# First norm of a hybrid encoder layer: the 16 modulation column tiles that it uses are summed over their inputs by TensorE in PSUM instead of by VectorE, ScalarE and Pool

## The chip, the core and the metric

The kernel runs on one core of one Trainium2 chip. A core has five engines that run their own instruction streams and meet at semaphores: TensorE (PE in the profile, its weight loads PEld), VectorE (DVE), ScalarE (ACT), GpSimd or Pool (POOL) and SyncE (SP), whose stream here issues most of the DMAs. The metric is the device time of one execution in microseconds; lower is better. The median of three runs of the kernel before is 2705.27 us (2701.91 to 2705.51).

## The reference

One layer of a bidirectional encoder on a sequence of 1024 tokens with 1024 features, float32. What the change touches is the first line of the layer: a modulation vector is computed from the condition `c`, and its first two sixths shift and scale the first norm. All four mixers start from `u`.

```python
cond = jax.nn.silu(c.astype(jnp.float32))              # (1, 1024)
mod = cond @ ada_w[l] + ada_b[l]                       # 1024 x 6144 weights
sh1, sc1, gt1, sh2, sc2, gt2 = jnp.split(mod[:, None, :], 6, axis=-1)
u = _rmsnorm(h, norm1_g[l]) * (1.0 + sc1) + sh1
p_rw, p_ml, p_lru, p_hg, p_gate = _split(u @ w_in[l], IN_SPLITS)
...
h = h + gt1 * (merged @ w_out[l])
u2 = _rmsnorm(h, norm2_g[l]) * (1.0 + sc2) + sh2
h = h + gt2 * _conv_ffn(u2, ...)
return _rmsnorm(h, final_g)
```

## The kernel before

Features lie on the 128 partitions, tokens along the free dimension. A column tile is 128 columns of `ada_w`, so `mod` is a tile of 128 partitions by 48 columns (column g holds column tile g: 0 to 7 are the shift, 8 to 15 the scale of the first norm). The condition after SiLU is `sc`, 128 by 8: column k holds inputs 128k to 128k+127.

The stage of the change is a loop of four steps (i = 0 to 3) in `run`. Step i makes the four column tiles 2i, 2i+1, 8+2i and 8+2i+1, and with them the feature tiles k = 2i and 2i+1 of `u`. In a step:

- `ada` loads, for two neighbouring column tiles at a time, all 1024 inputs of their 256 columns in one DMA of 1 MB (tile `ada_w`, 128 x 8 x 256). The weighted sum over the eight k is split: VectorE multiplies and accumulates k = 0 to 4 into one `ada_acc` (lines 1386 and 1388), ScalarE multiplies k = 5 to 7 (line 1397), and Pool adds these to a second `ada_acc` (line 1399).
- `ada_end` sums the 128 partitions of both accumulators with TensorE: the accumulator is the weight operand, a column of ones the moving one, and the result is one PSUM column (line 1414). VectorE adds the bias and writes `mod` (line 1417).
- `norm1` makes `g1` from `mod` and the norm's gain (lines 1459, 1460), transposes the normalised tokens `n1_x` for each k with TensorE (line 1446; first half to the PSUM bank `ps`, second half to `pt`), and scales and shifts out of PSUM into `n1_u`, first half by VectorE (1449), second by ScalarE (1451). ScalarE rounds this to `uh` (205), and VectorE or Pool takes the rest into `ul` (206).
- `proj_part` adds feature tiles to three column blocks of `u @ w_in` whose PSUM banks (`big`, `pc`, `pa`, `py`) stay open through the loop. Each product of two float32 matrices is three matmuls of 128 x 512 (lines 126 to 128: high by high, high by low, low by high), so that each k costs 18 matmuls: 144 in all.

The bank `pt` serves both `ada_end` and the second half of `norm1`; it has one buffer. After the loop come `load_cols`, `rw_params`, and then the first branch's projections with the LRU units (`lru`, `lru_unit`). Instructions are not in the order of the code: a list scheduler that runs when the kernel is built orders each engine's stream, so that a change in one stage also moves instructions in later ones. Matmul weights (`w_raw`) are split into `w_hi` (VectorE, line 119) and `w_lo` (Pool, line 120) through three buffers each.

Of the kernel before, what the change touches and what calls it, by code (L numbers as in the profile page):

```python
# [18 lines left out]
P = 128  # L19
T = 1024  # L20
ADD, SUB, MUL, MAX, MIN = ALU.add, ALU.subtract, ALU.mult, ALU.max, ALU.min


class K:
# [1351 lines left out]
    def ada(self, g0, g1, wp, G=4, bufs=2, ks=8, pend=None):  # L1376
# [3 lines left out]
        for g in range(g0, g1, G):  # L1380
# [24 lines left out]
            else:  # L1405
                pend.append((g, accs))

    def ada_end(self, pend, tag, G):
        nc = self.nc
        pt = self.ps([P, 512], tag)  # L1410
        for i, (g, accs) in enumerate(pend):
            for x in range(G):
                for q, acc in enumerate(accs):
                    nc.tensor.matmul(pt[:, G * i + x:G * i + x + 1], lhsT=acc[:, P * x:P * x + P], rhs=self.ones,
                                     start=(q == 0), stop=(q == len(accs) - 1))
        for i, (g, _) in enumerate(pend):
            nc.vector.tensor_tensor(self.mod[:, g:g + G], pt[:, G * i:G * i + G], self.c("ada_b", g, G), op=ADD)
# [48 lines left out]
    def run(self):  # L1466
        nc, a, tc = self.nc, self.a, self.tc
# [14 lines left out]
        with ExitStack() as es:  # L1482
            wp = es.enter_context(tc.tile_pool(name="st", bufs=1, reuse_waits="tile"))
            self.load_cols([("c", V("c")), ("ada_b", V("ada_b")), ("norm1_g", V("norm1_g"))], "D", wp)
            nc.scalar.activation(self.sc, self.c("c", 0, 8), AF.Silu)
            self.norm1_load(wp)
            self.ptags = [("big", "big"), ("pc", "pc"), ("pa", "py")]
            for i in range(4):
                pend = []
                with tc.high_priority(offset=self.AP):  # L1490
                    for g in (2 * i, 8 + 2 * i):
                        self.ada(g, g + 2, wp, 2, 8, self.ADK0, pend)
                    self.ada_end(pend, "pt", 2)
                ks = range(2 * i, 2 * i + 2)
                if i == 0:
                    self.norm1_stats(wp)
                    self.pres = [self.proj_start(self.win(c)) for c in (P * 12, 1792 + 1552, 1792 + 1552 + 512)]
                self.norm1(wp, ks)
                if i:
                    for pre in self.pres:  # L1500
                        self.proj_part(pre, self.PK)
                self.PK = ks
            self.load_cols([(n, V(n)) for n in ("norm2_g", "rw_mu", "rw_w0", "rw_a0", "rw_kk", "rw_ka")] +
                           [("rw_rk", a["rw_rk"].rearrange("o (j two) n -> (o j) (two n)", two=2))] +
                           [(n, V(n)) for n in ("rw_lnw", "rw_lnb", "ml_norm", "lru_conv_w", "lru_conv_b", "lru_ba",
                                                "lru_bx", "lru_lam", "hg_lb", "hg_norm")], "A", wp)
            fw = a["ffn_conv_w"].rearrange("o k (j p) -> o k j p", p=P)
            self.load_cols([("cw0", fw[0, 0]), ("cw1", fw[0, 1])], "B", wp)
            self.load_cols([("cw2", fw[0, 2]), ("cb", V("ffn_conv_b"))], "C", wp)
# [27 lines left out]
        with ExitStack() as es:  # L1537
            wp = es.enter_context(tc.tile_pool(name="hg", bufs=1, reuse_waits="tile"))
# [6 lines left out]
            for j in range(4):  # L1545
# [16 lines left out]
                for i in range(2):  # L1562
                    pt = self.ps([P, 4, P])
# [15 lines left out]
        with ml as es:  # L1579
# [8 lines left out]
            with ExitStack() as e2:  # L1588
                wp = e2.enter_context(tc.tile_pool(name="mlp", bufs=1, reuse_waits="tile"))
# [14 lines left out]
                w = self.wsplit_sb(wpad, 8)  # L1604
# [8 lines left out]
            wp = es.enter_context(tc.tile_pool(name="ml", bufs=1, reuse_waits="tile"))  # L1613
            self.filler = iter(())
            hs, q, kk = {}, {}, {}
# [50 lines left out]
        for n in (0, 3, 1, 2):  # L1666
# [6 lines left out]
            for jt in range(8):  # L1673
                sgt = self.t(mp, [P, T], "sgt", bufs=3)
                nc.sync.dma_start(out=sgt, in_=dG[8 * n + jt])
                w = self.wsplit(a["w_branch"][0, n, :, P * jt:P * jt + P], 4)
# [32 lines left out]
        wp = es.enter_context(tc.tile_pool(name="wo", bufs=1, reuse_waits="tile"))  # L1709
# [73 lines left out]
        wp = es.enter_context(tc.tile_pool(name="ffu", bufs=1, reuse_waits="tile"))  # L1783
# [147 lines left out]
        wp = self.pool("ff")  # L1931
# [22 lines left out]
        g = 0  # L1954
        while g + GR < NF:
            nx = [hidden(f) for f in range(g + GR, min(NF, g + 2 * GR))]
            down(g, GR, fs)
            fs, g = nx, g + GR
# [4 lines left out]
        w = []  # L1963
# [35 lines left out]
        pt = self.ps([P, 512])  # L1999
# [13 lines left out]
        for jt in range(8):  # L2013
# [9 lines left out]
            for k in range(jt if jt > 3 else 0, jt + 1) if jt >= 3 else ():  # L2023
                for i, (n, pt, ss) in enumerate(tl):
                    nc.tensor.matmul(ss[:, 0:1], lhsT=sqs[k][:, P * i:P * i + P], rhs=onesP, start=(k == 0), stop=(k == 7))
                    nc.tensor.matmul(pt[k // 4][:, P * (k % 4):P * (k % 4) + P], lhsT=hT[k][:, P * n:P * n + P],
                                     rhs=dg[:, k, :], start=True, stop=True)
# [88 lines left out]
```

## Time and profile before

| | us |
|---|---|
| median of three runs | 2705.27 (2701.91 to 2705.51) |
| the profiled execution, its own time | 2707.24 |
| its span (first to last instruction) | 2705.4 |
| TensorE busy in the span | 2501.7 (92%) |
| VectorE busy | 1768.4 (65%) |
| Pool busy | 1148.6 (42%) |
| ScalarE busy | 919.5 (34%) |

Shares over the whole span say little on one stage. The trace is therefore read in stretches, which are given from the start of the span: what each engine does there, what an engine waited for, and how fast TensorE's matmuls follow each other. TensorE runs at one of two clock levels; the column PEclk gives the granted share of the full one, and the step from one matmul's start to the next one's shows it too.

### The profile page before, as it was taken

To read this page: it belongs to the slowest core of one execution; us is meant where nothing else is said; L and a number is where in the kernel's file an instruction comes from. 1 tells how busy PE (TensorE), PEld (TensorE's weight loads), DVE (VectorE), ACT (ScalarE), POOL (GpSimd) and SP (SyncE) were. 2 spreads that over 40 slices of the span, in tenths; PEclk is the share of its full clock that TensorE was granted. 3 is DMA by queue.
4 is the path that set the end of the run, shared out by engine and by line. 5 is a ranking of instruction groups with operands and counts; after the bars stand their busy time and mean duration, and the time that the engine had idled before them with its cause. 6 is when DMAs were issued, how large, how long until landed. Compare 5 with 4: busy or idle time off the path is not lost.

```text
span 2705.4 us, 46888 instructions
## 1 busy us (share of the span) xinstructions
PE 2501.7 (92%) x18573; PEld 2010.5 (74%) x18573; DVE 1768.4 (65%) x2878; ACT 919.5 (34%) x1656; POOL 1148.6 (42%) x1150
## 2 busy tenths in 40 slices
PE   5999887899999999799989989999999999999998
PEld 4777666667777777588777777788777888888887
DVE  7667765776776652655563668367479999886344
ACT  4355542333333332343332342111235444442002
POOL 3654453433443323742221365367423444445332
PEclk9999998999999999899999989999999999999999
DMA  6422253444443423321111544555543222216222
GB/s 215 132 73 68 74 152 91 114 105 112 101 118 92 114 72 117 110 54 44 40 40 29 142 150 158 182 188 160 175 133 113 75 90 74 90 56 209 82 78 79
DMA packets 403173, 290.78 MB, mean 107 GB/s; under 512 B 121290, under 2 KB 365304, under 8 KB 402952
## 3 DMA queue, kind: packets, MB, share of 16 engines
q1 hardware_dynamic: 363976, 248.37, 31.7%
q10 hardware_dynamic: 38976, 39.40, 4.4%
q8 instruction: 146, 2.39, 0.4%
q14 instruction: 75, 0.61, 0.1%
HBM read 223.93 MB, written 63.77 MB: 106 GB/s over the span
## 4 chain that ended last, share of the span: by engine, by line
PE 53%; DVE 20%; issue 5%; DMA 3%; ACT 3%; POOL 2%; SPq 1%; ACTq 0%; DVEq 0%; POOLq 0%
PE pbig L126 8%; PE pbig L128 7%; PE pbig L127 7%; DVE rw_pr L1000 3%; PE ppc L128 2%; PE ppc L126 2%; PE ppc L127 2%; DVE s L1848 2%; PE ppy L126 1%; PE ppy L127 1%; PE ppy L128 1%; PE ppa L126 1%; PE ppa L127 1%; PE ppa L128 1%; DVE w_lo L1841 1%
## 5 line engine op out<-in xcount | busy, mean ns | idle before, releaser
L120 POOL TENSOR_TENSOR w_lo<-w_raw,w_hi 128x512 fp32r<-128x512 f32 x276 | 383.5, 1390 | 757.9 <-DVE w_hi L119 269.7
L126 PE MATMUL pbig<-uh,w_hi 128*128 128x512 f32 x1200 | 501.6, 419 | 20.4 <-ACT w_hi L117 8.5
L128 PE MATMUL pbig<-uh,w_lo 128*128 128x512 f32 x1200 | 479.1, 401 | 4.8 <-POOL w_lo L120 4.1
L127 PE MATMUL pbig<-ul,w_hi 128*128 128x512 f32 x1180 | 472.8, 401 | 0.0
L126 PEld LDWEIGHTS pbig<-uh,w_hi 128*128 128x128 f32 x1200 | 229.6, 192 | 86.5 <-ACT gt L1234 17.1
L128 PEld LDWEIGHTS pbig<-uh,w_lo 128*128 128x128 f32 x1200 | 230.4, 192 | 58.1 <-POOL w_lo L120 6.7
L127 PEld LDWEIGHTS pbig<-ul,w_hi 128*128 128x128 f32 x1180 | 227.2, 193 | 41.2 <-issue 1.1
L119 DVE CAST w_hi<-w_raw 128x512 fp32r<-128x512 f32 x216 | 135.3, 628 | 138.5 <-PE pbig L127 81.9
L128 PE MATMUL ppc<-uh,w_lo 128*128 128x512 f32 x352 | 139.3, 399 | 3.7 <-DVE w_lo L120 2.1
L126 PE MATMUL ppc<-uh,w_hi 128*128 128x512 f32 x352 | 138.3, 397 | 1.7 <-DVE w_hi L119 1.2
L127 PE MATMUL ppc<-ul,w_hi 128*128 128x512 f32 x332 | 131.1, 395 | 0.0
L126 PE MATMUL ppa<-uh,w_hi 128*128 128x512 f32 x216 | 86.2, 399 | 5.6 <-DVE w_hi L119 5.6
L128 PE MATMUL ppa<-uh,w_lo 128*128 128x512 f32 x216 | 85.4, 395 | 0.9 <-POOL w_lo L120 0.8
L126 PE MATMUL ppy<-uh,w_hi 128*128 128x512 f32 x216 | 85.7, 397 | 0.0
L128 PE MATMUL ppy<-uh,w_lo 128*128 128x512 f32 x216 | 84.8, 393 | 0.0
L117 ACT CAST w_hi<-w_raw 128x512 fp32r<-128x512 f32 x74 | 45.7, 618 | 112.3 <-PE pbig L127 52.0
L127 PE MATMUL ppa<-ul,w_hi 128*128 128x512 f32 x204 | 82.5, 404 | 0.0
L1839 ACT CAST w_hi<-s 128x512 fp32r<-128x512 f32 x80 | 49.4, 618 | 97.0 <-PE pbig L127 18.8
L127 PE MATMUL ppy<-ul,w_hi 128*128 128x512 f32 x208 | 82.2, 395 | 0.0
L128 PEld LDWEIGHTS ppc<-uh,w_lo 128*128 128x128 f32 x352 | 66.7, 190 | 20.8 <-DVE w_lo L120 2.6
L126 PEld LDWEIGHTS ppc<-uh,w_hi 128*128 128x128 f32 x352 | 67.1, 191 | 17.5 <-DVE w_hi L119 2.1
L1388 DVE SCALAR_TENSOR_TENSOR ada_acc<-ada_w,sc,ada_acc 128x256 f32<-128x256 f32 x112 | 71.9, 644 | 2.4
(790 smaller groups left out, 6219.1 us busy)
## 6 DMA issues: line engine op xcount, KB each, us to landing
w_raw<-in_w_in_dram SPq DMA_DIRECT2D x172, 256.0 KB
ada_w<-in_ada_w_dram SPq DMA_DIRECT2D x24, 1024.0 KB
s_raw<-in_ffn_up_dram SPq DMA_DIRECT2D x80, 256.0 KB
dG<-gt ACTq DMA_DIRECT2D x64, 256.0 KB
sgt<-dG SPq DMA_DIRECT2D x32, 512.0 KB
rw_in<-dIn SPq DMA_DIRECT2D x32, 384.0 KB
w_raw<-in_ffn_down_dram SPq DMA_DIRECT2D x44, 256.0 KB
dF<-cv SPq DMA_DIRECT2D x22, 512.0 KB
```

The source lines that it names most:

```text
L117: nc.scalar.copy(hi, raw[:, k0:k0 + m])
L119: nc.vector.tensor_copy(out=hi, in_=raw[:, k0:k0 + m])
L120: (nc.gpsimd if self.wlo == "p" else nc.vector).tensor_tensor(lo, raw[:, k0:k0 + m], hi.bitcast(F32), op=SUB)
L126: nc.tensor.matmul(pt, lhsT=wh, rhs=uh, start=start, stop=False)
L127: nc.tensor.matmul(pt, lhsT=wh, rhs=ul, start=False, stop=False)
L128: nc.tensor.matmul(pt, lhsT=wl, rhs=uh, start=False, stop=stop)
L1000: nc.vector.tensor_tensor(p4[:, y], l[:, y, i:i + m].unsqueeze(2).to_broadcast([64, m, n, n]), r[:, y].rearrange("p k j -> p j k").unsquee ...
L1388: nc.vector.scalar_tensor_tensor(acc, w[:, k, :], self.sc[:, k:k + 1], acc, op0=MUL, op1=ADD)
L1839: nc.scalar.copy(hi, x)
L1841: (nc.gpsimd if self.st_n % self.SL[1] < self.SL[0] else nc.vector).tensor_tensor(lo, x, hi.bitcast(F32), op=SUB)
L1848: (nc.gpsimd if i in self.SP else nc.vector).tensor_tensor(o, x, y, op=op)
```

## The change

The eight DMAs, `mod` and all that follows stay. The sums over k of the 16 column tiles are made by TensorE: the 128 x 128 block of `ada_w` for input tile k and a column tile is the weight operand, column k of `sc` is the moving one (128 x 1), and eight such matmuls add up in one PSUM column. The column-by-column work of VectorE, ScalarE and Pool and the sums with ones are gone for these tiles. The later 32 column tiles keep the old way.

```diff
+    def ada_pe(self, g, G, wp, pt):
+
+        nc = self.nc
+        w = self.t(wp, [P, 8, P * G], "ada_w", bufs=8)
+        nc.sync.dma_start(out=w, in_=self.a["ada_w"][0, :, P * g:P * (g + G)].rearrange("(k p) c -> p k c", p=P))
+        for x in range(G):
+            for k in range(8):
+                nc.tensor.matmul(pt[:, x:x + 1], lhsT=w[:, k, P * x:P * x + P], rhs=self.sc[:, k:k + 1],
+                                 start=(k == 0), stop=(k == 7))
+        nc.vector.tensor_tensor(self.mod[:, g:g + G], pt[:, :G], self.c("ada_b", g, G), op=ADD)
...
             for i in range(4):
-                pend = []
                 with tc.high_priority(offset=self.AP):
-                    for g in (2 * i, 8 + 2 * i):
-                        self.ada(g, g + 2, wp, 2, 8, self.ADK0, pend)
-                    self.ada_end(pend, "pt", 2)
+                    pt = self.ps([P, 512], "pt")
+                    for q, g in enumerate((2 * i, 8 + 2 * i)):
+                        self.ada_pe(g, 2, wp, pt[:, 4 * q:])
```

In the changed kernel the lines behind the new function have numbers that are larger by 11: the transposes of line 1446 stand at 1457, `mod` of the new function at 1417. On TensorE, at the end of step 0's first transposes (`pps` is the bank `ps`, `ppt` the bank `pt`), stand before:

```order
L1446 MATMUL pps_229<-ident_73,n_x_33_112 128x128
L1414 MATMUL ppt_153<-ones_79,ada_acc_39_127 128x1
L1414 MATMUL ppt_153<-ones_79,ada_acc_40_133 128x1
L1414 MATMUL ppt_153<-ones_79,ada_acc_39_127 128x1
L1414 MATMUL ppt_153<-ones_79,ada_acc_40_133 128x1
L1414 MATMUL ppt_153<-ones_79,ada_acc_42_141 128x1
L1414 MATMUL ppt_153<-ones_79,ada_acc_43_147 128x1
L1414 MATMUL ppt_153<-ones_79,ada_acc_42_141 128x1
L1414 MATMUL ppt_153<-ones_79,ada_acc_43_147 128x1
L1446 MATMUL ppt_235<-ident_73,n_x_34_113 128x128
```

and in the changed kernel at the same place:

```order
L1457 MATMUL pps_229<-ident_73,n_x_33_112 128x128
L1415 MATMUL ppt_125<-sc_78,ada_w_126 128x1 x16
L1415 MATMUL ppt_125<-sc_78,ada_w_145 128x1 x16
L1457 MATMUL ppt_235<-ident_73,n_x_34_113 128x128
L1457 MATMUL ppt_235<-ident_73,n_x_35_114 128x128
```

Two bursts of 16 matmuls, one for each DMA, take the place of eight matmuls, and the same transposes follow. In step 1 the eight matmuls of line 1414 stand nearly together behind `pps_300`; in the changed kernel the first burst stands there, and the second one inside the projections, here with its neighbours:

```order
L126 MATMUL ppc_223<-uh_12_82,w_hi_349 128x512
L127 MATMUL ppc_223<-ul_20_90,w_hi_349 128x512
L1415 MATMUL ppt_258<-sc_78,ada_w_278 128x1 x16
L128 MATMUL ppc_223<-uh_12_82,w_lo_350 128x512
L127 MATMUL ppa_224<-ul_19_89,w_hi_367 128x512
```

In steps 1 to 3 each step has on TensorE, in this order, 6 matmuls of line 126, a burst, 19 matmuls of lines 126 to 128, a burst, 11 more, and 16 transposes. Further on, where the first branch and the LRU unit begin, VectorE's stream is also in another order. Before, from the first `lru_a` to the third weight tile `w_hi_1096`:

```order
L815 CAST lru_a_201_777<-lru_th_200_774 128x1024
L262 SCALAR_TENSOR_TENSOR lru_xc_836<-lru_xb_798,colsA_635,lru_xc_836 128x1024
L732 TENSOR_TENSOR rw_kk_734<-rw_kk_734,rw_q_735 128x1024
L815 CAST lru_a_204_789<-lru_th_203_786 128x1024
L119 CAST w_hi_1023<-w_raw_1021 128x512
L262 SCALAR_TENSOR_TENSOR lru_xc_836<-lru_xb_798,colsA_635,lru_xc_836 128x1024
L203 CAST lru_w_210_841<-lru_w_830 128x512
L119 CAST w_hi_1090<-w_raw_1088 128x512
L806 TENSOR_TENSOR lru_s_199_767<-rw_kk_734,lru_s_198_766 128x1024
L228 TENSOR_TENSOR lru_e_757<-lru_e_757,lru_m_758 128x8
L229 TENSOR_SCALAR lru_C_759<-lru_e_757 128x8
L119 CAST w_hi_1096<-w_raw_1094 128x512
```

and in the changed kernel:

```order
L815 CAST lru_a_185_777<-lru_th_184_774 128x1024
L262 SCALAR_TENSOR_TENSOR lru_xc_836<-lru_xb_798,colsA_635,lru_xc_836 128x1024
L815 CAST lru_a_188_789<-lru_th_187_786 128x1024
L262 SCALAR_TENSOR_TENSOR lru_xc_836<-lru_xb_798,colsA_635,lru_xc_836 128x1024
L119 CAST w_hi_1023<-w_raw_1021 128x512
L732 TENSOR_TENSOR rw_kk_734<-rw_kk_734,rw_q_735 128x1024
L203 CAST lru_w_194_841<-lru_w_830 128x512
L806 TENSOR_TENSOR lru_s_183_767<-rw_kk_734,lru_s_182_766 128x1024
L228 TENSOR_TENSOR lru_e_757<-lru_e_757,lru_m_758 128x8
L119 CAST w_hi_1090<-w_raw_1088 128x512
L229 TENSOR_SCALAR lru_C_759<-lru_e_757 128x8
L119 CAST w_hi_1096<-w_raw_1094 128x512
```

The same twelve instructions stand in both; the second weight tile `w_hi_1090` has moved behind `lru_s` and `lru_e`, and the last row is the same.

## Rows read from the trace of the kernel before

**Rows 1.** The page: busy time, share of the span and instructions.

```profile
PE 2501.7 (92%) x18573; PEld 2010.5 (74%) x18573; DVE 1768.4 (65%) x2878; ACT 919.5 (34%) x1656; POOL 1148.6 (42%) x1150
```

**Rows 2.** Groups of instructions, 25 to 80 us: busy us, mean ns, idle before.

```profile
L1388 DVE SCALAR_TENSOR_TENSOR ada_acc<-ada_w,sc,ada_acc 128x256 f32<-128x256 f32 x32 | 22.6, 713 | 0.7
L1399 POOL TENSOR_TENSOR ada_acc<-ada_acc,ada_w 128x256 f32<-128x256 f32 x16 | 12.8, 804 | 24.1 <-ACT ada_w L1397 23.5
...
L1386 DVE TENSOR_SCALAR ada_acc<-ada_w,sc 128x256 f32<-128x256 f32 x8 | 3.7, 466 | 0.0
```

**Rows 3.** Timeline: start, duration, engine, instruction, wait and its releaser; step 0.

```profile
25.19 0.51 ACT L1397 ACTIVATE ada_acc<-ada_w,sc 128x256 f32<-128x256 f32 x1 [0.84 <-DMA ada_w<-in_ada_w_dram]
...
28.21 0.51 ACT L1397 ACTIVATE ada_acc<-ada_w,sc 128x256 f32<-128x256 f32 x1 [1.72 <-DMA ada_w<-in_ada_w_dram]
...
31.65 1.78 PEld L1414 LDWEIGHTS ppt<-ones,ada_acc 128*128 128x128 f32 x8 [1.25 <-DVE ada_acc L1388]
...
34.03 0.21 DVE L1417 TENSOR_TENSOR mod<-ppt,colsD 128x2 f32<-128x2 f32 x2
...
35.52 0.78 ACT L1451 ACTIVATE n_u<-ppt,mod,g 128x512 f32<-128x512 f32 x1
...
36.33 1.05 ACT L205 CAST uh<-n_u 128x1024 fp32r<-128x1024 f32 x1
...
37.57 1.20 PE L126 MATMUL pbig<-uh,w_hi 128*128 128x512 f32 x2
```

**Rows 4.** Timeline of TensorE: ones-matmuls of steps 1, 2 and 3.

```profile
40.77 1.62 PE L1414 MATMUL ppt<-ones,ada_acc 128*128 128x1 f32 x14
...
56.75 1.87 PEld L1414 LDWEIGHTS ppt<-ones,ada_acc 128*128 128x128 f32 x16
...
69.44 1.88 PE L1414 MATMUL ppt<-ones,ada_acc 128*128 128x1 f32 x16
```

**Rows 5.** Timeline: TensorE's waits in the stage, and matmuls of 128 x 512.

```profile
50.81 1.09 PE L1446 MATMUL ppt<-ident,n_x 128*128 128x128 f32 x4 [2.63 <-DVE mod L1417]
...
68.88 0.50 PE L126 MATMUL ppa<-uh,w_hi 128*128 128x512 f32 x1 [0.48 <-DVE w_hi L119]
...
71.76 0.63 PE L128 MATMUL pbig<-uh,w_lo 128*128 128x512 f32 x1
72.19 0.63 PE L127 MATMUL pbig<-ul,w_hi 128*128 128x512 f32 x1
...
88.57 0.39 PE L127 MATMUL ppa<-ul,w_hi 128*128 128x512 f32 x1
...
89.25 0.40 PE L128 MATMUL ppy<-uh,w_lo 128*128 128x512 f32 x1
```

**Rows 6.** Stretches, TensorE alone: length, busy us, PEclk, DMA share, GB/s.

```profile
50.00:60.00 10.00, 9.19 (x50) 0.83 0.04 11
...
70.00:80.00 10.00, 10.00 (x48) 0.83 0.21 54
71.00:72.00 1.00, 1.00 (x5) 0.55 0.77 191
```

**Rows 7.** Stretches of small matmuls later: busy PE, PEld, DVE, ACT, POOL, PEclk.

```profile
1592.00:1596.00 4.00, 4.00 (x16) 3.32 (x16) 1.15 (x4) 1.93 (x3) 0.48 (x1) 0.50 0.32 87
...
1600.00:1604.00 4.00, 4.00 (x17) 3.32 (x17) 1.70 (x3) 0.81 (x2) 1.29 (x2) 0.50 0.65 204
```

**Rows 8.** Line 1414's instructions: count, duration ns least/median/greatest.

```profile
L1414 PEld LDWEIGHTS ppt<-ones,ada_acc x64: 187/192/339, 28.6 to 71.0; 128*128 128x128 f32 x64
```

**Rows 9.** Timeline, TensorE and VectorE, where the first branch begins.

```profile
95.95 1.00 DVE L259 TENSOR_SCALAR lru_xc<-lru_xb,colsA 128x1024 f32<-128x1024 f32 x1 [5.58 <-POOL lru_xb L237]
...
111.07 0.41 DVE L119 CAST w_hi<-w_raw 128x512 fp32r<-128x512 f32 x1
...
111.62 0.47 PE L126 MATMUL ppa<-uh,w_hi 128*128 128x512 f32 x1 [4.01 <-DVE w_hi L119]
...
117.13 0.41 DVE L119 CAST w_hi<-w_raw 128x512 fp32r<-128x512 f32 x1
```

## Prediction

> **What bounds the kernel now.** The page comes first: TensorE is busy in 92% of the span, VectorE in 65% [rows 1]. That says only that time given to TensorE is likely to show at the end. The stage of the change has to be read alone, because there the shares are others.
>
> The groups of instructions from 25 to 80 us give the work that the change removes: VectorE spends 22.6 + 3.7 = 26.3 us on the sums over k, Pool 12.8 us [rows 2]. Pool's price does not matter, since it waited 24.1 us for ScalarE in the same rows. VectorE's matters only where TensorE waited for it, which the timeline tells. In step 0 it did: two DMAs land at 25.2 and 28.2, the sums end, TensorE adds up the partitions, and `mod` is written at 34.03; ScalarE's share of `u` starts at 35.52, `uh` at 36.33, and the first matmul of the projections at 37.57 [rows 3]. In the three other steps TensorE waited 2.63 us for step 1's `mod`, and 0.48 us for a weight tile [rows 5]. That is all that it waited there for longer than a few tenths: the last matmul of the three projections starts at 89.25 [rows 5], so the stage from first to last matmul takes 52.1 us, and TensorE fills it but for those 3.1 us.
>
> It does not fill it at one rate. Matmuls of 128 x 512 follow each other at 0.68/3 = 0.227 us at 88.57 to 89.25, but at 0.43 us at 71.76 [rows 5]; the granted clock reads 0.55 from 71 to 72 and 0.83 over each of the stretches 50 to 60 and 70 to 80 [rows 6]. A mean of 0.83 over 10 us is 3.4 us at half rate, the lower of the two levels (1.2 instead of 2.4 GHz), and 1.7 us lost, twice. In step 0 I go by the steps from one weight load to the next: eight in 1.78 us are 0.222 us each [rows 3], against 1.87/16 = 0.117 us at 56.75 [rows 4]. That is the lower level too.
>
> So the stage is TensorE's, with one early wait for VectorE. The change takes the work from the engine that has room and gives it to the one that has little.
>
> **The change part by part.**
>
> *Price of a burst.* The new matmul has the form of the old one with ones: 128 x 128 float32 weights, 128 x 1 moving. The trace counts 64 records of line 1414 for the 32 matmuls of this stage [rows 8], two each; a burst of 16 matmuls is 32 records. At the full level that is 32 x 0.117 = 3.74 us, at the lower one 32 x 0.222 = 7.12 us. The weight load sets it: its duration goes from 187 to 339 ns [rows 8], and a column of output costs next to nothing.
>
> Here a rule says less. The Trainium skill (TensorE: Matmul & The Clock Gate, LDWEIGHTS) puts a weight load at its 128 columns over 1.2 GHz, about 107 ns, whatever the array does; by that a burst would be an estimated 3.4 us at either level and the sum below about 9 us smaller. This trace disagrees at the lower level, with 0.222 us a step.
>
> *Step 0.* TensorE has idled before 25.2 and is at the lower level, where it was in the same place before. Two bursts are 14.24 us. The second one's first matmul also waits for VectorE's addition of the first one's bias (both write one PSUM tile), which costs about what lies between the old loads' end, 31.65 + 1.78 = 33.4, and `mod` [rows 3]: 0.6 us, and 0.6 us more to the second `mod`. So `mod` comes at 25.2 + 14.24 + 1.2 = 40.6 instead of 34.03: **+6.6**. The bounds are nothing gained on the lower rate, and the full rate for both bursts (2 x 3.38 us less). What is queued behind `mod` on VectorE is `g1`, `n_u` and `ul`, and TensorE's transposes into `pt` wait for it; the 3.54 us from `mod` to the first projection matmul [rows 3] stay.
>
> *Steps 1 to 3.* Six bursts at the full level, 22.4 us, in place of three times 1.87 us [rows 4]: **+16.8**. The data are there: the first two DMAs land 3.0 us apart [rows 3], so the eighth lands near 25.2 + 7 x 3 = 46, before TensorE comes to it.
>
> *Waits that go.* 2.63 and 0.48 us [rows 5]: **-3.1**. The first is VectorE's lateness; the second came of a crowded VectorE.
>
> *A wait that comes.* With each second burst behind 19 projection matmuls, the 16 transposes of a step come last, and only then ScalarE can scale and round. That chain is 37.57 - 35.52 = 2.05 us [rows 3], and TensorE has but twelve transposes for it, two fours of which wait for ScalarE's and VectorE's reads themselves. I take 0.9 us each, between nothing and the 2.05: **+2.7**.
>
> *The clock.* This is the term with the widest bounds. I count the two half-rate stretches of before as gone, 2 x 1.7 us, and put what replaces them into the price of the bursts: **-3.4**. What a burst does to the clock: the ones-matmuls at 40.77 and 56.75 [rows 4], half a burst, were followed by projections at the full step; those at 69.44, behind a short wait [rows 5], by the fall at 71 [rows 6]. Later, from 1592 to 1596 and again from 1600 to 1604, TensorE was busy without a gap with small matmuls, its weight loads taking 3.32 of 4 us, and the clock stayed at 0.50 [rows 7]. So a busy TensorE whose time goes into weight loads does not get the clock up. I take it that every burst, twice as long as the one at 69.44, costs a fall. A first burst of a step has 19 projection matmuls behind it and costs what that fall did, 1.7 us. A second one has only 11, then transposes, a wait, six matmuls and the next burst: that is the mixture of step 0, which stayed at the lower level throughout. The bounds are 1.7 and 1.7 + 3.4 (the next burst at the lower rate too); I take 2.9. Together 3 x 1.7 + 3 x 2.9: **+13.8**, between 0 and 30.
>
> *Behind the stage.* The streams are reordered up to the recurrent branch. TensorE waits 4.01 us at 111.62 for the second weight tile; VectorE makes that at 111.07 and the third at 117.13 in a chain that starts at 95.95 with data of the projections [rows 9]. The second tile now stands later in VectorE's stream, TensorE has other matmuls ahead of it, and the third has the same work ahead. I take nothing, with 4 us either way, the size of that wait. The whole chain hangs on the projections, so that it moves with them and takes nothing of the delay back.
>
> Sum: 6.6 + 16.8 - 3.1 + 2.7 - 3.4 + 13.8 = **+33.4 us**. The profiled execution took 2707.24 us (1.8 beside its span), so it would be 2740.6; the median of the runs lies 2.0 below it. I predict **2739 us**.
>
> **The rivals.**
>
> 1. *The bursts leave the clock up* (or even raise it). For it: 40.77 and 56.75 [rows 4]. Against it: 69.44, and the long stretch at 0.50 [rows 7]. Without the 13.8 the sum is +19.6, 2725 us. If the first two bursts also ran at the full rate (2 x 3.38 us less), it is +12.8, 2718 us. The Trainium skill (TensorE: Matmul & The Clock Gate, Why this matters for your kernels) asks for a TensorE that is kept busy without idle gaps, and by that rule a burst would hold the clock as well as any matmul. Rows 7 show no gap and a low clock.
>
> 2. *The clock stays down through the whole stage.* Each of six bursts costs 3.38 + 1.7 us, 30 instead of 13.8: +49.6, 2755 us. Step 0 speaks for it; the projections of before speak against it, since the clock came up among them in both stretches [rows 6].
>
> 3. *Not slower: a matmul costs one record instead of two.* The moving operand is now real data and not ones, and the weights come straight from a DMA. If the pair of passes shrank to one, the six bursts would cost 11.2 us less, the first two 7.1 us less, and as each burst would be no longer than that at 40.77, the clock's 13.8 would go too: 33.4 - 32.1 = +1.3, 2707 us. It decides where 19.6 falls to 5.4, which is at 0.61 of the price, a step of 0.072 instead of 0.117 us. Against it: both operands are float32 as before, and the old matmuls took two records each [rows 8].
>
> **How the numbers follow.** The forecast, slower with falls of the clock, has 0.68, and its own range is 2726 to 2748. Rival 1 has 0.17, rival 2 has 0.10, rival 3 has 0.05. The range of 8 in 10 is 2718 to 2752: it takes in rival 1 and the order's 4 us, and leaves out rival 3 and most of rival 2. A measurement can tell about 0.2%, 5.4 us. Faster 0.02, within 0.2% 0.05, slower 0.93; the 0.05 comes of rival 3 and of rival 1 with a lucky order.
>
> **What would show it.** `mod` of step 0 at 40 to 41 us, with records of line 1415 at 0.22 us; 256 records in all; a granted clock of 0.5 behind most bursts; the last matmul of the projections at about 89.25 + 33 = 122 instead of 89.25, and the same distance from there to the end as before, within 4 us. I am wrong if that matmul comes before 105, if the bursts run at 0.117 us with the clock at 1.00, or if the distance from there to the end changes by more than the order's 4 us.

## The result, and the profile after

The changed kernel takes 2735.47 us (median of four runs, 2733.26 to 2743.97), the kernel before beside it 2705.39. The ratio is 1.0114, with a 95% interval of 1.0097 to 1.0132. The forecast was 2739 us, slower, with a range of 2718 to 2752. The profiled execution took 2735.21 us, 28.0 more than that of before, against the +33.4 of the sum.

The page, first row, shows the trade ([rows 1]): TensorE has 37.5 us more to do, VectorE 22.9 less.

```profile
PE 2539.2 (93%) x18765; PEld 2045.8 (75%) x18765; DVE 1745.5 (64%) x2838; ACT 907.9 (33%) x1632; POOL 1134.3 (41%) x1134
```

The new line's instructions (duration ns least/median/greatest, first and last start) answer to [rows 8]: two records to each of the 128 matmuls, a weight load of 187 to 338 ns as before.

```profile
L1415 PEld LDWEIGHTS ppt<-sc,ada_w x256: 187/192/338, 25.1 to 103.7; 128*128 128x128 f32 x128
L1415 PE MATMUL ppt<-sc,ada_w x256: 164/250/373, 25.1 to 103.7; 128*128 128x1 f32 x128
```

The timeline of step 0 answers to [rows 3]. Each burst takes 7 us, 0.22 us a record, and `mod` is complete at 39.35 instead of 34.03. The first projection matmul starts at 42.63 instead of 37.57.

```profile
25.11 6.96 PE L1415 MATMUL ppt<-sc,ada_w 128*128 128x1 f32 x32 [5.97 <-DMA ada_w<-in_ada_w_dram]
32.11 0.16 DVE L1417 TENSOR_TENSOR mod<-ppt,colsD 128x2 f32<-128x2 f32 x1 [6.97 <-PE ppt L1415]
32.32 6.99 PE L1415 MATMUL ppt<-sc,ada_w 128*128 128x1 f32 x32 [0.25 <-DVE mod L1417]
39.35 0.16 DVE L1417 TENSOR_TENSOR mod<-ppt,colsD 128x2 f32<-128x2 f32 x1 [7.08 <-PE ppt L1415]
...
42.63 0.79 PE L126 MATMUL pbig<-uh,w_hi 128*128 128x512 f32 x1
```

TensorE's timeline of the rest of the stage answers to [rows 4, 5]. A burst costs 3.63 us where the clock stays up through it, and 4.85 where it falls inside; behind the one at 45.11 the projections go at 0.43 us a matmul (50.40 to 50.83). The last projection matmul starts at 118.79 instead of 89.25: **+29.5 us at the end of the stage**.

```profile
45.11 4.85 PE L1415 MATMUL ppt<-sc,ada_w 128*128 128x1 f32 x32
...
50.40 0.63 PE L128 MATMUL pbig<-uh,w_lo 128*128 128x512 f32 x1
50.83 0.63 PE L127 MATMUL pbig<-ul,w_hi 128*128 128x512 f32 x1
...
56.22 3.63 PE L1415 MATMUL ppt<-sc,ada_w 128*128 128x1 f32 x32
...
118.79 0.39 PE L128 MATMUL ppy<-uh,w_lo 128*128 128x512 f32 x1
```

Stretches of TensorE (length, busy us, PEclk, DMA share, GB/s) around the first of these bursts, as in [rows 6]: no idle time, and the granted clock at its lower level, 0.50, for over six microseconds.

```profile
46.00:48.00 2.00, 2.00 (x17) 0.82 0.03 7
48.00:50.00 2.00, 2.00 (x11) 0.50 0.04 11
50.00:52.00 2.00, 2.00 (x5) 0.50 0.16 45
52.00:54.00 2.00, 2.00 (x6) 0.50 0.00 0
54.00:56.00 2.00, 2.00 (x11) 0.97 0.00 0
```

What TensorE waited for from 40 us to the end of the stage (total, times, longest): little.

```profile
PE ppt L1457 <- ACT n_u L1462: 1.1, 3, 0.4
PE ppt L1457 <- DVE mod L1417: 0.3, 1, 0.3
PE pbig L126 <- ACT uh L205: 0.2, 1, 0.2
```

### The profile page after: what moved, and what is told of

Read it like the earlier page. It is cut to its first block, busy times and chain, and to the rows that moved or that the text cites. A ratio compares the mean times of both kernels' runs of the same rounds, so it can differ in the third digit from the quotient of the medians.

```text
span 2733.4 us, 47194 instructions
## 1 busy us (share of the span) xinstructions
PE 2539.2 (93%) x18765; PEld 2045.8 (75%) x18765; DVE 1745.5 (64%) x2838; ACT 907.9 (33%) x1632; POOL 1134.3 (41%) x1134
## 4 chain that ended last, share of the span: by engine, by line
PE 51%; DVE 20%; issue 5%; DMA 3%; ACT 3%; POOL 1%; SPq 1%; DVEq 0%; ACTq 0%; POOLq 0%
PE pbig L126 8%; PE pbig L127 7%; PE pbig L128 7%; DVE rw_pr L1000 3%; PE ppc L128 2%; PE ppc L126 2%; PE ppc L127 2%; DVE s L1858 2%; PE ppy L127 1%; PE ppy L128 1%; PE ppy L126 1%; PE ppa L127 1%; PE ppa L126 1%; DMA rw_pr<-dA 1%; PE ppa L128 1%
## 5 line engine op out<-in xcount | busy, mean ns | idle before, releaser
L127 PEld LDWEIGHTS ppc<-ul,w_hi 128*128 128x128 f32 x332 | 63.4, 191 | 13.8 <-issue 0.2
```

Source lines behind the costliest of these rows:

```text
L127: nc.tensor.matmul(pt, lhsT=wh, rhs=ul, start=False, stop=False)
```

## The experiments

The runs of the kernel before beside the experiments scatter more than those above (2697.34 to 2719.83), so that whole times tell a few microseconds badly. Each kernel is therefore also read at the stage's end: the start of the last of the 144 projection matmuls, 89.25 us in the kernel before. "Lost" is what the lower clock level cost there: the length of the stretch from 46 us to that matmul times one minus its granted clock; in s123, row0 and row0w, whose first fall comes earlier, it is counted from 42 us. The clock is read to 0.01, so that "lost" is good to a few tenths of a microsecond (twice: about 0.7). The column PEclk reads 1.00 ahead of the first fall in a trace, also where the steps show the lower level, so that it can't be used for step 0. All columns but the ratio are read from one execution of each kernel. The kernels are named by their labels.

| kernel | ratio to before, 95% interval | `mod` of step 0 | first projection | last projection | against before | lost |
|---|---|---|---|---|---|---|
| before | 1 | 34.03 | 37.57 | 89.25 | | 3.4 |
| changed | 1.0114 (1.0097 to 1.0132) | 39.35 | 42.63 | 118.79 | +29.5 | 13.4 |
| again: changed, once more | 1.0082 (1.0058 to 1.0105) | 39.37 | 42.65 | 112.53 | +23.3 | 7.0 |
| s0: step 0 alone | 1.0044 (1.0025 to 1.0063) | 40.66 | 44.73 | 91.84 | +2.6 | 0.0 |
| s123: steps 1 to 3 alone | 1.0073 (1.0049 to 1.0096) | 32.96 | 36.37 | 110.04 | +20.8 | 10.2 |
| k0: bursts of 2 matmuls | 0.9966 (0.9950 to 0.9982) | 29.06 | 32.34 | 81.38 | -7.9 | 1.8 |
| twice: bursts of 32 | 1.0304 (1.0275 to 1.0333) | 52.79 | 56.07 | 178.94 | +89.7 | 40.9 |
| row: operands swapped | 1.0059 (1.0036 to 1.0081) | 35.87 | 38.82 | 110.09 | +20.8 | 1.9 |
| spread: no bursts, same matmuls | 1.0060 (1.0043 to 1.0076) | 39.03 | 42.44 | 108.10 | +18.9 | 0.0 |
| g0: one pair of step 0 | 0.9996 (0.9980 to 1.0012) | 34.86 | 40.12 | 88.70 | -0.6 | 1.7 |
| g2: one pair of step 1 | 1.0052 (1.0026 to 1.0079) | 33.16 | 38.27 | 92.35 | +3.1 | 3.4 |
| warm: TensorE busy before 25 us | 1.0126 (1.0104 to 1.0148) | 37.96 | 41.24 | 116.78 | +27.5 | 11.9 |
| row0: step 0 alone, swapped | 0.9994 (0.9981 to 1.0007) | 37.59 | 41.74 | 91.05 | +1.8 | 3.4 |
| row0w: the same, TensorE busy before | 1.0010 (0.9997 to 1.0023) | 37.11 | 41.26 | 88.20 | -1.1 | 0.5 |

The rows behind "lost", one stretch of TensorE (length, busy us, PEclk, DMA share, GB/s) from each of the traces of the changed kernel, the changed kernel once more, spread, row and k0, in this order; that of s123 starts at 42 us, where its first burst stands, and is the sixth, and the last one is that of twice:

```profile
46.00:110.00 64.00, 62.85 (x332) 0.79 0.06 15
```

```profile
46.00:110.00 64.00, 62.31 (x358) 0.89 0.07 19
```

```profile
44.00:108.00 64.00, 61.06 (x384) 1.00 0.10 28
```

```profile
46.00:110.00 64.00, 60.17 (x283) 0.97 0.09 25
```

```profile
46.00:82.00 36.00, 33.07 (x159) 0.95 0.18 49
```

```profile
42.00:110.00 68.00, 66.60 (x354) 0.85 0.12 34
```

```profile
46.00:178.00 132.00, 130.40 (x618) 0.69 0.05 12
```

**Half of the change: s0 and s123.** The loop keeps the old way in the other steps; s123 has `i > 0`.

```diff
+                pend = []
...
-                    pt = self.ps([P, 512], "pt")
-                    for q, g in enumerate((2 * i, 8 + 2 * i)):
-                        self.ada_pe(g, 2, wp, pt[:, 4 * q:])
+                    if i == 0:
+                        pt = self.ps([P, 512], "pt")
+                        for q, g in enumerate((2 * i, 8 + 2 * i)):
+                            self.ada_pe(g, 2, wp, pt[:, 4 * q:])
+                    else:
+                        for g in (2 * i, 8 + 2 * i):
+                            self.ada(g, g + 2, wp, 2, 8, self.ADK0, pend)
+                        self.ada_end(pend, "pt", 2)
```

> Only step 0 is summed by TensorE; steps 1 to 3 are summed the old way, by VectorE, ScalarE and Pool. Theory A (the added time is a late `mod` of step 0, the TensorE time of six bursts, and falls of the clock behind those six) expects `mod` of step 0 at 39.4 us as in the changed kernel, +5.1 us from it, no falls of the clock beyond the two of before, and, as VectorE is free of step 0's sums, at most the 2.6 us wait of step 1 gone: +2 to +5 us against before, some 25 us under the changed kernel. Theory B (step 0 sets the clock for the whole stage: the two bursts there keep it from coming up in time, and what is lost later follows from that) expects the falls to stay without the six later bursts: +12 to +18 us.

> Step 0 is summed the old way, steps 1 to 3 by TensorE. Theory A expects `mod` of step 0 at 34 us as before, six bursts of some 3.7 us less three times 1.87 (+16.8), the falls of the clock behind them (+13.7 less the 3.4 of before), the wait of 2.6 us for step 1's `mod` gone and 1.3 us of new waits: +24 to +26 us against before, and together with the kernel that has only step 0 by TensorE about the +30 of the whole change. Theory B expects the falls gone with step 0's bursts: +12 to +15 us.

At the stage's end s0 is 2.6 us late and has no fall at all; its first projection matmul is 7.2 us late, and 4.6 of that come back, since step 1's wait for `mod` [rows 5] and the two falls of before [rows 6] are gone. s123 has the falls without step 0's bursts. Theory B falls with both. s123 lies 3 to 5 us below what A expected, and the two halves add up to +23.4: 6 us less than the first trace of the changed kernel, and just what the other one (below) has.

The whole time of s0 says +12 us (1.0044), not +2.6. In its trace the rest, +6.8, comes together behind 388 us, where the code is the same and the granted clock loses no more than in the kernel before (75.5 against 77.5 us, summed over 4 us stretches of the whole span). What brings these microseconds was not settled. g2 also gets later behind the stage (+3.1 at its end, +14.8 in the span), but there the clock accounts for it: by the same sum it loses 91.9 us, 14.4 more than before, and its five executions have a granted clock of 0.966 to 0.970, where the 22 of before beside them have 0.967 to 0.975. Why a single burst should be followed by falls so far behind it is not shown.

**The size of a burst: k0 and twice.** The first edit below is that of twice, the second that of k0.

```diff
-            for k in range(8):
+            for k in [*range(8), *range(8)]:
```

```diff
-            for k in range(8):
-                nc.tensor.matmul(pt[:, x:x + 1], lhsT=w[:, k, P * x:P * x + P], rhs=self.sc[:, k:k + 1],
-                                 start=(k == 0), stop=(k == 7))
+            nc.tensor.matmul(pt[:, x:x + 1], lhsT=w[:, 0, P * x:P * x + P], rhs=self.sc[:, 0:1],
+                             start=True, stop=True)
```

> The sum takes only k = 0: a burst is two matmuls instead of 16, seven eighths of the sum over the inputs are left out; DMAs, bias, order and waits stay. It leaves the moved work's price on TensorE out and keeps all that the change takes from VectorE, ScalarE and Pool. Theory A (price and clock follow from the length of the bursts) expects `mod` of step 0 near 29.5 us instead of 34.0 (-4.5), 0.9 us of TensorE less in each later step (-2.8), the waits of 3.1 us gone, the two falls of before gone (-3.4) and 1.3 us of new waits: -10 to -13 us against before, some 42 under the changed kernel. Theory C (the falls come from any small matmuls set into the projections, or from the transposes and waits at a step's end, whatever the bursts' length) expects the clock's 13.7 us still there: +2 to +6 us.

> Each burst is run over twice, so that its matmuls are 32 instead of 16 and the last one's sum holds each product twice. Theory A (a long run of small matmuls brings the clock down, so that what is added runs at the lower level) expects step 0's `mod` 14 us later and six more burst lengths of up to 7.1 us instead of 3.7: +50 to +57 us against the changed kernel, with a granted clock of 0.50 in the second half of a burst. Rival D (a burst costs its weight loads at the full level, and the clock's falls are there whatever its length) expects 14 + 6 x 3.74: +36 us.

(In twice the second pass starts its sum anew, so that it only repeats the first; the expectation says otherwise.) TensorE's timeline of k0 shows step 0 with bursts of 1 us, the second as soon as its DMA lands:

```profile
25.01 0.98 PE L1414 MATMUL ppt<-sc,ada_w 128*128 128x1 f32 x4 [5.94 <-DMA ada_w<-in_ada_w_dram]
28.04 0.98 PE L1414 MATMUL ppt<-sc,ada_w 128*128 128x1 f32 x4 [2.05 <-DMA ada_w<-in_ada_w_dram]
```

k0 keeps 1.8 us of the falls, so theory C (any small matmuls among the projections) falls too. Its -7.9 us at the stage's end is what all the work taken from VectorE, ScalarE and Pool is worth if TensorE gets it for almost nothing. That is less than the 10 to 13 us expected: `mod` of step 0 came as forecast (29.06), but TensorE waits 3.3 us in the stage, 2.1 of them for VectorE's `n_u`, where 1.3 us of waits were expected, and one fall is left. In twice step 0's `mod` comes 13.4 us later than in the changed kernel (forecast 14), and the projections take 46.7 us more from first to last, where six more bursts at the full rate would be 6 x 3.63 = 21.8. The rest is the clock: it loses 40.9 instead of 13.4 us. The timeline shows a burst of twice that starts at the full step and ends at the lower one (52 records before the next projection matmul, of 64; 5.9 us at the full step of 0.113 us, 8.27 here):

```profile
59.35 8.27 PE L1415 MATMUL ppt<-sc,ada_w 128*128 128x1 f32 x52
67.48 0.77 PE L127 MATMUL pbig<-ul,w_hi 128*128 128x512 f32 x1
```

Theory A stands and was still low (+60.2 at the stage's end, expected 50 to 57); rival D with +36 falls.

**What a burst is made of, and that it is one: row and spread.** In row the eight matmuls of a DMA have `sc` as weights and 256 moving columns; in spread one matmul of a burst stands behind each projection matmul.

```diff
-        for x in range(G):
             for k in range(8):
-                nc.tensor.matmul(pt[:, x:x + 1], lhsT=w[:, k, P * x:P * x + P], rhs=self.sc[:, k:k + 1],
-                                 start=(k == 0), stop=(k == 7))
+                nc.tensor.matmul(row[0:1, sl], lhsT=self.sc[:, k:k + 1], rhs=w[:, k, :], start=(k == 0), stop=(k == 7))
+            nc.scalar.copy(r[:, sl], row[0:1, sl])
...
+        for x in range(4):
+            nc.tensor.matmul(pt[:, x:x + 1], lhsT=r[0:1, P * x:P * x + P], rhs=self.ones[0:1, 0:1], start=True, stop=True)
```

```diff
+                        for n in range(len(pm)):
+                            ops.append(pm[n])
+                            if 2 <= n < 34:
+                                ops.append(am[n - 2])
+                        self.in_row(ops)
```

> The operands of the bursts change places: the column of `sc` is the weight and 256 columns of `ada_w` are the moving operand, eight matmuls for each DMA instead of 16, whose sum is a row of 256 in PSUM; ScalarE copies the row to SBUF and four matmuls of one partition turn it into columns in each step. TensorE's time for the products is about the same at the full level (16 records at about the 0.21 us step of 256-wide float32 matmuls in the trace of before), but a record streams 256 columns instead of one. Theory A in the form that the clock falls because a burst is nearly all weight load and few columns expects the falls behind the bursts gone or nearly so: about -10 to -14 us against the changed kernel for the clock, with 1 to 2 us back for the turn into columns and ScalarE's copies: +16 to +22 us against before. Rival E (the falls come with the order that the change makes, the breaks in the projections and the waits at a step's end, and not with what the bursts are made of) expects a clock as in the changed kernel: +28 to +33 us against before.

> The matmuls of the bursts in steps 1 to 3 are the same, but each stands between two projection matmuls instead of behind its like; step 0 is as in the changed kernel. Theory A in the form that a burst without many columns brings the clock down expects the falls of the clock gone: 13.7 us less than the changed kernel at best, +16 to +20 us against before. If what counts is the share of weight loads over a longer stretch, and not the burst, the clock falls for as long or longer: as slow as the changed kernel or some us slower, +28 to +40 us against before.

TensorE's timeline of row, step 0. The first burst's 16 records begin at the lower step, 0.42 us, and the clock rises within it (5.15 us); the second one takes 3.61, 0.226 us a record. The changed kernel's two bursts of one column, twice as many records, stay at the lower level to their end.

```profile
25.11 5.15 PE L1418 MATMUL ppt<-ada_w,sc 128*1 128x256 f32 x16 [5.94 <-DMA ada_w<-in_ada_w_dram]
30.72 3.61 PE L1418 MATMUL ppt<-ada_w,sc 128*1 128x256 f32 x16 [0.45 <-ACT ada_r L1419]
```

And of spread, step 1. A pair of records stands between two projection matmuls, and the pair of steps is 45.25 to 45.71, 0.46 us: 0.228 for the projection and 0.114 for each record, no more than in a burst.

```profile
45.25 0.28 PE L1414 MATMUL ppt<-sc,ada_w 128*128 128x1 f32 x2
45.39 0.48 PE L1418 MATMUL ppa<-uh,w_hi 128*128 128x512 f32 x1
45.71 0.28 PE L1414 MATMUL ppt<-sc,ada_w 128*128 128x1 f32 x2
```

Both lose next to nothing to the clock, and both end where they were forecast. Rival E falls: the order and the waits are there in row too. With the same matmuls and weight loads in spread, what brings the clock down is that they stand together; in row, where the operands are swapped, bursts that stand together do not. Nor is this the chance of one trace: the granted clock of the whole span is 0.969 to 0.974 in the eight executions of spread and 0.971 to 0.975 in the four of row, but 0.962 to 0.968 in all eight of the changed kernel. row gets back less than it saves on the clock because it adds work: four turns into columns of 1.05 us, and 4.2 us of waits for `n_u`, `mod` and `uh` behind 38 us, where the changed kernel has the 1.6 us above. Their ratios (1.0059 and 1.0060) lie below both of the changed kernel (1.0114 and 1.0082), but the intervals overlap that of the second, so that the whole time alone would not settle it.

**One burst: g0 and g2.** Only one pair of column tiles goes to `ada_pe`, the other seven the old way.

```diff
+    PEG = (0,)
...
+                        if g in self.PEG:
+                            self.ada_pe(g, 2, wp, pt[:, 4:])
+                        else:
+                            self.ada(g, g + 2, wp, 2, 8, self.ADK0, pend)
```

> Only the column pair of step 0's first DMA is summed by TensorE, which has nothing else to do then, while VectorE, ScalarE and Pool sum the pair of the second DMA; all other pairs are summed the old way. Theory A (TensorE's time counts from its first projection matmul on, and VectorE's where TensorE waits for it) expects the burst of 7.0 us from 25.1 to 32.1 hidden beside VectorE's sums for the second DMA, `mod` of step 0 no later than before, VectorE free about 3.3 us earlier, and so the 2.6 us wait for step 1's `mod` and perhaps one fall of the clock less: -2 to -5 us against before. Rival F (the wait of step 1 is set by the DMAs or by the order, not by VectorE's backlog, or the burst delays step 0's transposes) expects 0 to +3 us.

> Only the pair of step 1's first DMA is summed by TensorE, all other pairs the old way: one burst, where the matmuls with ones for that pair are gone. Theory A expects the burst's 3.74 us less half of 1.87, one fall of the clock of up to 2.9 us, and against it the wait of 2.6 us for step 1's `mod` gone: 0 to +4 us against before. Rival G (a single burst leaves the clock up, and only the repeated ones bring it down) expects 0 to -1 us.

g0 is no change. VectorE's timeline shows why: its first sum is at 28.00, where it has to wait for the second DMA, and step 1's `mod` is written at 50.88, where it was at 50.45.

```profile
28.00 0.35 DVE L1387 TENSOR_SCALAR ada_acc<-ada_w,sc 128x256 f32<-128x256 f32 x1 [2.88 <-DMA ada_w<-in_ada_w_dram]
...
50.88 0.21 DVE L1429 TENSOR_TENSOR mod<-ppt,colsD 128x2 f32<-128x2 f32 x2
```

The time that VectorE was spared it stood idle, and sums for step 1 in front of `g1` and `n_u` ate the rest: the first projection matmul is 2.6 us later than before. Theory A was wrong here, and rival F is the nearer one, by the order of VectorE's stream. The 0.6 us gained at the stage's end are less than the 1.7 by which the clock lost less. g2 has one burst, and a fall that begins at its end; TensorE's timeline goes on at 0.43 us a matmul. So a single burst can be followed by a fall, against rival G; but in all g2 loses 3.4 us of the stage, no more than the kernel before, and with one trace the price of a single burst is not settled.

```profile
43.59 3.82 PE L1416 MATMUL ppt<-sc,ada_w 128*128 128x1 f32 x32
47.27 0.77 PE L126 MATMUL pbig<-uh,w_hi 128*128 128x512 f32 x1
47.84 0.63 PE L127 MATMUL pbig<-ul,w_hi 128*128 128x512 f32 x1
48.27 0.63 PE L128 MATMUL pbig<-uh,w_lo 128*128 128x512 f32 x1
```

**The rate of step 0's bursts, and a way to use TensorE there: warm, row0 and row0w.** warm and row0w have twelve more matmuls; row0 is row in step 0, the old way in the others.

```diff
+                        for n in (1, 2, 3, 4, 5, 5):
+                            wm = self.ps([P, 512], "pc")
+                            for _ in range(2):
+                                nc.tensor.matmul(wm, lhsT=self.ident, rhs=self.n1x[n][:, :512], start=True, stop=True)
```

> The changed kernel with twelve matmuls of 128 x 512 columns before 25 us, whose results nobody reads, where TensorE otherwise idles. If step 0's bursts run at the lower level because TensorE idled before them, the first of them takes about 3.7 instead of 6.96 us, the second 3.7 to 7 (the clock may fall in it, as behind the later bursts), `mod` of step 0 comes at 33 to 36 instead of 39.35 us, and the end of the stage moves 3 to 6 us ahead of the changed kernel's. If a burst runs at the lower level because of what it is made of, whatever goes before, both stay at 7 us and nothing moves.

> Step 0 alone is summed by TensorE, with the operands changed about (`sc` as the weight, 256 columns of `ada_w` moving); steps 1 to 3 are summed the old way. From the two runs that it combines (with only step 0 by TensorE the projections took 47.1 us from first to last matmul; with the operands changed about everywhere the first one stood at 38.8 us): the last projection matmul at 85.9 instead of 89.25 us, -3.3 us against before at the end of the stage. The rival: the lead does not last, as the projections' 47.1 us came of step 0's delay, in which VectorE got ahead with step 1's sums, and 1 us of it is lost for each us by which step 0 is earlier: 0 at the end of the stage.

> Step 0 alone by TensorE with the operands changed about, as in the run beside it, and the same twelve matmuls before 25 us. If these bring the clock up, the first burst takes 3.6 instead of 5.15 us, the second starts when its DMA lands, `mod` of step 0 comes at about 34.2 instead of 35.9 us, and the last projection matmul at about 84.2 us: -5 us against before at the end of the stage. The rival: as in the run beside it the lead is lost to VectorE's sums for step 1, 0 at the end of the stage.

TensorE's timeline of warm: behind the matmuls of 512 columns the first burst takes 3.63 us instead of 6.96, so the lower rate at which it starts in the changed kernel came of what TensorE did before. The second one takes 5.63: the granted clock reads 0.95 from 32 to 34 us and 0.50 from 34 on.

```profile
21.54 7.03 PE L1511 MATMUL ppc<-n_x,ident 128*128 128x512 f32 x16
28.41 3.63 PE L1415 MATMUL ppt<-sc,ada_w 128*128 128x1 f32 x32
32.29 5.63 PE L1415 MATMUL ppt<-sc,ada_w 128*128 128x1 f32 x32 [0.25 <-DVE mod L1417]
```

The twelve matmuls last until 28.4, 3.3 us longer than I had sized them, and so `mod` is only 1.4 us earlier; the last projection is 2.0 us earlier than in the first trace of the changed kernel (3 to 6 were expected), which is less than two traces of it differ.

Neither row0 nor row0w beats the kernel before (0.9994 and 1.0010, both intervals around 1). The lead is lost, but not first to VectorE's sums, as the rivals had it: it is lost on ScalarE. Its timeline in row0 shows the copy of the second row at 35.51, though TensorE ended that burst at 34.62: step 1's DMA had landed, and ScalarE's products for step 1 stand ahead of the copy. `mod` comes at 37.59 instead of 35.87.

```profile
34.30 0.51 ACT L1397 ACTIVATE ada_acc<-ada_w,sc 128x256 f32<-128x256 f32 x1 [1.70 <-DMA ada_w<-in_ada_w_dram]
34.71 0.89 ACT L1397 ACTIVATE ada_w<-ada_w,sc 128x256 f32<-128x256 f32 x2
35.51 0.34 ACT L1419 COPY n_u<-ppt 1x256 f32<-1x256 f32 x1
```

**The changed kernel once more: again.** No edit.

> The changed kernel itself once more, on the chip of the other runs. If the falls of the clock follow from the bursts, the stage ends within 2 us of 118.8 us again and its falls stand behind the same bursts; if they are chance, the falls stand elsewhere and the stage's end moves by 4 us or more. Whole time: +25 to +33 us against before.

The stage ends at 112.53, 6.3 us ahead of the first trace, and loses 7.0 instead of 13.4 us to the clock: the difference is the clock. TensorE's timeline shows both bursts of step 1 at the full rate and the projections between them at 0.23 us, where the first trace had one of its two longest falls:

```profile
45.03 3.63 PE L1415 MATMUL ppt<-sc,ada_w 128*128 128x1 f32 x32
...
48.85 0.39 PE L128 MATMUL pbig<-uh,w_lo 128*128 128x512 f32 x1
49.08 0.39 PE L127 MATMUL pbig<-ul,w_hi 128*128 128x512 f32 x1
...
52.96 3.63 PE L1415 MATMUL ppt<-sc,ada_w 128*128 128x1 f32 x32
```

So not every burst costs a fall, and which one does differs between executions of the same program. The expectation left this as chance, and that is what it is in part (whether both executions ran on the same chip is not known). What holds over all traces: with the six bursts the stage lost 13.4, 7.0, 10.2 and 11.9 us (changed, again, s123, warm); without them, or with their matmuls spread or their operands swapped, 0 to 3.4. The spans of the two traces differ by only 1.3 us (2733.4 and 2732.1), so most of the 6 us went again in later stages: over the whole span the second trace loses 94.3 us to the clock, the first 89.5. The whole time, +22 us by the ratio, is below the +25 to +33 expected.

## Why the prediction was right, step by step

The forecast, slower with falls of the clock, came true, and the whole was 3.5 us high (2739 against 2735.47). That it is so near is luck in part: the clock's term fits the first trace and not the second, and the same kernel once more is 22 us above before, where the sum has 33.4. By its terms:

- *Step 0, +6.6*: the first projection matmul came 5.1 us later. The bursts ran at the lower level as said (6.96 and 6.99 instead of 7.12 each); the two waits for VectorE's addition were mis-sized, one of 0.25 us and next to nothing instead of 1.2 together, since VectorE had nothing else to do. That the first burst ran at the lower rate because TensorE had idled is shown by warm; that it did not rise through both goes with what they are made of, since in row it rose within the first.
- *Steps 1 to 3, +16.8*, *waits that go, -3.1*, *a wait that comes, +2.7*: without the lower level, the projections of before take 51.68 - 3.4 = 48.3 us from first to last matmul, those of the two traces 76.16 - 13.4 = 62.8 and 69.88 - 7.0 = 62.9. That is +14.6, where these terms sum to +16.4. The wait that comes is mis-sized: the rows above have 1.1 us for ScalarE, not 2.7. A burst at the full rate takes 3.63 us, not 3.74, which is 0.7 for six. Together that would be 14.1, half a microsecond less than measured.
- *The clock, +13.8 and -3.4*: 13.4 us in the profiled execution, 7.0 in the other trace. The mechanism, that bursts of weight loads bring the clock down, is shown by k0, twice, row and spread. The size was right for one execution and is above all four (13.4, 7.0, 10.2 and 11.9). The way it was divided is wrong: a first burst of a step was to cost 1.7 us and a second 2.9, from the transposes and waits behind it. In the profiled execution the falls at the first bursts cost 3.4, 1.7 and 3.4 us, those behind the second ones 1.7 each (sums over the 2 us stretches), and in the second trace step 1's first burst cost none.
- *Behind the stage, 0 ± 4*: the span is 28.0 us longer, the stage 29.5, so 1.5 us came back; in the second trace 3.5 us were added. Both are within the 4 us. TensorE's timeline has a wait of 0.51 us for a weight tile where one of 4.01 was [rows 9], and a new one of 2.91 for the LRU's weights:

```profile
120.78 0.47 PE L126 MATMUL ppc<-uh,w_hi 128*128 128x512 f32 x1 [0.51 <-DVE w_hi L119]
...
137.79 0.47 PE L126 MATMUL pps<-lru_x,lru_w 128*128 128x512 f32 x1 [2.91 <-DVE lru_w L203]
```

  It is not a mere shift, though: around 388 us of before some matmuls are 20.3 us late and others 25.1, and the end 28.0.

The rivals: (1), the clock stays up, did not happen in this kernel; what it would have cost spread shows, +18.9 us at the stage's end against the +19.6 of its sum. (2), down throughout, is what no trace of this kernel shows, and twice comes nearest; (3), one record for a matmul, is excluded by the 256 records. Of what was to be seen, the last projection matmul at 122 came at 118.79 and 112.53, and `mod` at 39.35, below the 40 to 41.

The Trainium skill (TensorE: Matmul & The Clock Gate, LDWEIGHTS) gives a weight load as its columns over 1.2 GHz, an estimated 107 ns for 128, with one value for both levels of the clock. Here such a load takes 187 to 338 ns, and the step from one to the next goes with the granted clock, 0.113 us at the full level and 0.22 at the lower one. The advice of the Trainium skill (TensorE: Matmul & The Clock Gate, Why this matters for your kernels), no idle gaps on TensorE, did not keep the clock up here: the bursts and the projections behind them have none from 46 to 56 us, and the clock fell.

## What to carry to other kernels

Work that cost 7.9 us of the stage on engines with room (what k0 gained by unloading them) cost 18.9 us net on the engine that bounds the stage, with its clock up, and 4 to 11 more with the bursts that bring the clock down. A matrix-vector product on TensorE is paid by its weight loads: if it must go there, spread its matmuls between wide ones, or make the vector the weight and the matrix the moving operand. And read a stage's end in two executions before a term of some microseconds is believed, because a good match may be luck.

## What the runs showed of the hardware that was not expected

- The granted clock falls at different places in two executions of the same program: the stage lost 13.4 us in one and 7.0 in the other.
- TensorE's clock rose inside a burst of 16 float32 records of 256 columns (5.15 us, the next one 3.61), but through 64 records of one column, 14 us long, it stayed at the lower level.
- A small matmul between two wide ones costs no more than in a burst: 0.114 us a record against 3.63/32 = 0.113.
